# Hybrid decoder block on one core: the room of part 2's small tiles, the MLP's first loads, and where the left operands' combinations are made

## The chip, the core and the metric

The kernel runs on one core of a Trainium2 chip. Its time is the device time of one execution in microseconds (us); a kernel is run several times and the median is given. Five engines work side by side, each on its own queue and in order: TensorE (PE, matmuls into PSUM), VectorE (DVE), ScalarE (ACT), GpSimd (POOL) and SyncE (SP), which here issues all DMAs. They wait for each other through semaphores only.

## The reference

One decoder block on x of 2048 tokens by 1024, float32:

```python
h = _rmsnorm(x, norm_pre_mix)
proj = einsum('bsd,de->bse', h, w_in)          # q, k, v, u, z, two gates
y_attn = _mixer_dilated_attention(q, k, v)     # three dilated windows, softmax-combined
y_gmlp = _mixer_chunked_gmlp(u, z, ...)        # causal mixing in chunks of 128 tokens
merged = gate_a * (y_attn @ w_branch_attn) + gate_b * (y_gmlp @ w_branch_gmlp)
y = merged @ w_out
x = x + _rmsnorm(y, norm_post_mix)
h = _rmsnorm(x, norm_pre_mlp)
a = relu(h @ w_mlp_in)                         # 1024 -> 4096
y = (a * a) @ w_mlp_out                        # 4096 -> 1024
x = x + _rmsnorm(y, norm_post_mlp)
```

## The kernel before

**Numbers.** A float32 operand is split into a high part, rounded to TensorE's `float32r`, and the rest (`split`, lines 66 to 74: ACT, POOL or DVE writes the high part, DVE or POOL subtracts, L75). A product is three matmuls: high by high, high by low, low by high.

**Order.** TensorE's instructions run in the order in which the program writes them (`manual_schedule`). For the other engines and the DMA queue a planner lays out the order with a model of the times; on the chip each queue then runs strictly in that order. A tile that takes the room of older tiles waits for those tiles' last users.

**Part 1** (lines 127 to 715) computes the projections, the attention and the gMLP and leaves them in DRAM: `gate_d`, `ya_d`, `yg_d`. Its last matmuls on TensorE are the z products, which read the second of two `hT` buffers.

**Part 2** (718 to 1037) goes over four chunks of 512 tokens in the order 2, 3, 0, 1. `load_y` loads and splits the chunk's six y tiles. `merge` makes, for each of eight slices dt, two products with `w_branch`, multiplies them by the sigmoid of the gates (`gt`, L753), adds them (POOL, L755) and splits the sum into `mg`. `out_block` multiplies four blocks of 128 tokens by `w_out` (`wo`), adds the residual (`xr`, stored as `x1_d`) after one norm, applies the next norm with the gains `gpost` and `gmlp` (`y1`, L790 to L800), and at its next call (`flush`) transposes the result. Chunks 2 and 0 store the transposes as `h2_d`; chunks 3 and 1 combine them with those of the partner chunk (POOL, L814 to L817) and store five tiles per block, `t_d` (L821, `store`). For chunk 1 these tiles lie in `tail`, which takes the place of the y tiles.

**The MLP** uses Strassen-Winograd's scheme: seven products in place of eight on 2x2 blocks, `TERMS` naming the left and right operand of each. It has two stages.

*First stage* (line 1040 on): for two halves of the tokens and 16 quarters q of `w_mlp_in`, `product` makes seven products of 12 matmuls each. The right operands are `B11`, `B21` (from `h2_d`) and `T1` to `T4`, `B22` (from `t_d`, `load_t`); they stay for a half. The left ones come from pairs of raw tiles `w1r` (`load_a`), combined on POOL and split (`sum_a`: S1 to S4 and A22 into tiles `wl`), or, for the first four and the last three q, as lone halves `ar` (`lone_a`, tag `c`). `places` orders the products: near the ends of a half all products 1 and 2 come ahead, then chains of 6, 7, 5, 4, 3. The results are squared, and at product 3 POOL makes four more combinations (L955 to L961), the left operands of the second stage; seven tiles per (half, q) are stored in `s_d`, laid out as 7 x 128 columns for each block of 128 tokens.

*Second stage* (1101 on): 64 steps n (8 groups g of two q, by 8 blocks), each of seven products of 6 matmuls (`yproduct`). `load_s` loads and splits the two 7 x 128 tiles of a step two steps ahead, in three sets of buffers; `load_w2`, `sum_w2` and `op_w2` make the right operands of the next group in 18 buffers (4 in `r4`, 14 in `bL`). DVE adds each result to the accumulators `acc` (L1204). In the last group `finish` normalizes a chunk's block, adds the residual and stores the output.

**Room.** Pools are stacked. Part 2's pools `yp2`, `gtp`, `mg0`, `wop`, `y1p`, `sm2`, `mg1`, `tp2` all belong to `e2`, which closes after the last block's store (L1045). Only then do the MLP's `bp` (right operands), `wp3` and `cp3` open, over the same room; the second stage's `bL` and `yp3` follow over these.

Of the kernel before, what the change touches and what calls it, by code (L numbers as in the profile page):

```python
# [41 lines left out]
def block_kernel(ctx, tc, a, out):  # L42
# [78 lines left out]
    s_d = dtile([NF // 2, 2, P, 4, 7, P], "sd")  # L121
# [596 lines left out]
    e2 = ExitStack()  # L718
    yp = stack(e2, "yp2", 1)
# [3 lines left out]
    y1p = stack(e2, "y1p", 2)  # L723
    sm = stack(e2, "sm2", 2)
    wo = [wop.tile([P, 2, D], F32R, name=f"wo{k}") for k in range(KT)]

    def load_wo(k):
        raw = y1p.tile([P, D], F32, name=f"woraw{k}", tag="y1")
        split_in(wo[k], a["w_out"][:, k, :], raw, "act")

    def load_y(c, engs=("act", "dve")):
        cs = slice(c * 512, (c + 1) * 512)
        yt = yp.tile([P, 6, 2, 512], F32R, name=f"yt{c}", tag="yt")
        for k in range(6):
            split_in(yt[:, k], ya_d[k, :, cs] if k < 2 else yg_d[k - 2, :, cs], None, *engs)
        return yt

    def merge(c, yt, between, each=None):
        cs = slice(c * 512, (c + 1) * 512)
        mg = []  # L740
        for dt in range(KT):
# [4 lines left out]
            for wch, ks in ((0, range(0, 2)), (1, range(2, 6))):  # L746
# [4 lines left out]
                for k in ks:  # L751
                    mm3(p, wb[k][:, 0, dsl], wb[k][:, 1, dsl], yt[:, k, 0, :], yt[:, k, 1, :], k == ks[0], k == ks[-1])
# [10 lines left out]
    def out_block(c, i, mg):  # L763
# [3 lines left out]
        xt = tp.tile([P, D], F32, name=f"xr_{c}{i}", tag="xr", bufs=1)  # L767
        sp.dma_start(xt, x[t0:t0 + P, :])
        second = c % 2
        if second:  # L770

            tt = tt_tile(c, i)
            for o in range(2):
                sp.dma_start(tt[:, 3 * o], h2_d[:, o * 4:o * 4 + 4, t0 - 512:t0 - 512 + P])
        y1 = y1p.tile([P, D], F32, name=f"y1_{c}{i}", tag="y1")
# [26 lines left out]
        for k in range(0, KT, 4):  # L802
            pt = psum_aux(f"pt_{c}{i}{k}")
            if second:
                ht = tt[:, 4 if k else 2]
# [7 lines left out]
        if second:  # L813
            pool.tensor_sub(tt[:, 0], tt[:, 2], tt[:, 0])  # L814
            pool.tensor_sub(tt[:, 1], tt[:, 4], tt[:, 0])
            pool.tensor_sub(tt[:, 2], tt[:, 4], tt[:, 2])
            pool.tensor_sub(tt[:, 3], tt[:, 3], tt[:, 1])  # L817
        yield
        if second:
            dst = t_d[c // 2].rearrange("p o k t -> p (o k) t")[:, :, i * P:(i + 1) * P]  # L820
            sp.dma_start(dst, tt.rearrange("p o k t -> p (o k) t"))  # L821
# [14 lines left out]
    chunks = (2, 3, 0, 1)  # L836
    e3, er = ExitStack(), ExitStack()
# [11 lines left out]
    b_, a_, araw, bank, xs_, u_, c1_ = {}, {}, {}, {}, {}, {}, {}  # L849
# [40 lines left out]

    def sum_a(half, q):
# [4 lines left out]
        w = {n: wp3.tile([P, 2, 4, P], F32R, name=f"{n}_{half}{q}", tag="wl", bufs=7) for n in names}  # L896
        s1 = wp3.tile([P, 4, P], F32, name=f"s1_{half}{q}", tag="s1", bufs=2)
# [9 lines left out]
    def product(half, q, i):  # L907
# [25 lines left out]
        elif i == 2:  # L933
            c1_[key] = rx.tile([P, 512], F32, name=f"c11_{nm}", tag="c1", bufs=LEAD + 1)
            square(c1_[key], p)
            store_s(0, c1_[key])
        elif i in (6, 7):
            u_[half, q, i] = cp3.tile([P, 512], F32, name=f"u{i}_{nm}", tag=f"u{i}", bufs=3 if i == 6 else 2)
            dve.tensor_add(u_[half, q, i], xs_[key], p)

# [4 lines left out]
        if i in (5, 7) and (half, q, "c") in bank and (half, q, 7) in u_:  # L945
            output(u_[half, q, 7], bank[half, q, "c"])
            store_s(5, u_[half, q, 7])
# [3 lines left out]
        elif i == 3:  # L951
            a11, a12, a21, a22 = c1_[key], xs_[key], u_[half, q, 6], u_[half, q, 7]
            output(a21, p)
            s1, s2, s4 = (cp3.tile([P, 512], F32, name=f"s{n}_{nm}", tag="c", bufs=3) for n in (1, 2, 4))
            pool.tensor_add(s1, a21, a22)  # L955
            store_s(4, s1)
            pool.tensor_sub(s2, s1, a11)
# [34 lines left out]
    def spatial_out(dt):  # L992

        nonlocal tp, gpost, gmlp, ttp
        if dt < 2:
            sz_out(*late.pop(0))
        if dt == 1:
            ez.close()
            mgp.append(stack(e2, "mg1", 1))
            tp = stack(e2, "tp2", 2)  # L1000
            gpost = tp.tile([P, D], F32, name="gpost", bufs=1)
# [294 lines left out]
```

## Time and profile before

| | |
|---|---|
| median of 3 runs | 2868.62 us (2867.49 to 2871.62) |
| the profiled execution | 2863.28 us, span 2861.5 us, mean granted TensorE clock 0.977 |
| busy, share of the span | PE 95%, DVE 55%, ACT 36%, POOL 35% |
| moved by DMA | 475 MB, mean 166 GB/s |

The span goes from the first to the last instruction of one profiled execution. A row of busy time by stretches gives, for each engine, its busy microseconds and its number of instructions in the stretch; then TensorE's granted clock as a share of full speed, the DMA engines' busy share and the GB/s moved. Matmuls overlap in the record, so TensorE's rate is read from the number of matmuls in a stretch rather than from its busy time. A row of the list of waits names the engine and line that waited, what released it, and total, times and longest in us. SPq is SyncE's queue: the row tells when a DMA was issued and how long its issue took, waiting for its turn included.

### The profile page before, as it was taken

What the parts mean: (1) busy time and instruction counts of PE and PEld (TensorE: products, weight loads), DVE (VectorE), ACT (ScalarE), POOL (GpSimd) and SP (SyncE); (2) the same over time, 40 slices, a digit from 0 to 9 for tenths busy, and PEclk for the clock granted to TensorE, in tenths of its full rate; (3) what the DMA queues carried; (4) which work ended last, traced back from release to release, by engine and by line L of the source; (5) the groups of instructions that cost most, each with busy time, mean ns of one, the idle gap of its engine ahead of it and who ended that gap; (6) DMA issues with size and microseconds to landing.
All of it is one profiled execution on the core that took longest, in us unless ns stands there. A gap on an engine that the chain in (4) does not pass through costs nothing. (4 is left out here: it accounts for less than half of the span.)

```text
span 2861.5 us, 36328 instructions
## 1 busy us (share of the span) xinstructions
PE 2729.3 (95%) x13364; PEld 2287.1 (80%) x13364; DVE 1587.3 (55%) x2684; ACT 1039.1 (36%) x2039; POOL 1003.7 (35%) x703
## 2 busy tenths in 40 slices
PE   8999999999999999999996999899997999999996
PEld 8889888988888888787775788677886887888875
DVE  5664462444443353655556544555445676777788
ACT  4213111244443321543444454454444222223332
POOL 0340341200000023213025665546658343344434
PEclk9999999999999999999998999989999999999998
DMA  7544545465666464656467555655556323333345
GB/s 252 176 150 149 173 135 180 142 201 177 203 210 199 163 199 128 204 171 183 143 186 234 155 158 159 191 174 157 157 156 209 117 95 125 126 120 125 127 137 196
DMA packets 348370, 475.38 MB, mean 166 GB/s; under 512 B 19872, under 2 KB 222880, under 8 KB 348192
## 3 DMA queue, kind: packets, MB, share of 16 engines
q1 hardware_dynamic: 348192, 473.06, 52.0%
q8 instruction: 105, 1.72, 0.2%
q14 instruction: 73, 0.60, 0.1%
HBM read 307.11 MB, written 165.87 MB: 165 GB/s over the span
## 5 line engine op out<-in xcount | busy, mean ns | idle before, releaser
L70 ACT ACTIVATE s<-s 128x896 fp32r<-128x896 f32 x128 | 121.9, 953 | 269.8 <-PE ya L1197 137.8
L918 PE MATMUL aa<-B,A 128*128 128x512 f32 x768 | 191.2, 400 | 11.6 <-ACT A L70 9.3
L1204 DVE TENSOR_TENSOR acc<-acc,ya 128x512 f32<-128x512 f32 x224 | 151.4, 683 | 80.2 <-PE ya L1197 79.7
L75 DVE TENSOR_TENSOR s<-s 128x896 fp32r<-128x896 f32 x128 | 169.5, 1326 | 44.6 <-ACT s L70 44.4
L918 PEld LDWEIGHTS aa<-B,A 128*128 128x128 f32 x768 | 146.5, 192 | 47.5 <-ACT A L70 10.5
L72 POOL TENSOR_SCALAR w_g<-w_g_r 128x1024 fp32r<-128x1024 f32 x32 | 34.2, 1068 | 411.2 <-PE g L87 384.8
L85 PE MATMUL x<-hT_a,wq 128*128 128x512 f32 x384 | 149.7, 390 | 0.0
L87 PE MATMUL x<-hT_a,wq 128*128 128x512 f32 x384 | 149.4, 389 | 0.0
L86 PE MATMUL x<-hT_a,wq 128*128 128x512 f32 x384 | 149.4, 389 | 0.0
L603 DVE TENSOR_REDUCE o<-po 128x256 f32<-128x512 f32 x48 | 33.2, 691 | 183.9 <-PE po L602 183.9
L918 PE MATMUL ab<-T_first,S 128*128 128x512 f32 x384 | 96.7, 402 | 24.2 <-ACT T_first L70 15.9
L70 ACT ACTIVATE hl<-r 128x512 fp32r<-128x512 f32 x48 | 30.4, 633 | 231.5 <-POOL r L248 86.7
L1197 PE MATMUL ya<-T2y,s 128*128 128x512 f32 x384 | 100.0, 396 | 13.8 <-ACT s L70 13.8
L75 POOL TENSOR_TENSOR T2y<-w2r,T2y 128x512 fp32r<-128x512 f32 x16 | 20.5, 1306 | 262.4 <-ACT T2y L70 262.4
L1197 PE MATMUL ya<-B11y,s 128*128 128x512 f32 x384 | 103.0, 405 | 9.9 <-DVE acc L1204 9.9
L75 DVE TENSOR_TENSOR A<-w1r,A 128x512 fp32r<-128x512 f32 x68 | 64.8, 953 | 84.5 <-ACT A L70 84.4
L899 POOL TENSOR_TENSOR s<-w1r 128x512 f32<-128x512 f32 x32 | 43.8, 1369 | 191.6 <-DMA w1r<-in_w_mlp_in_dram 183.8
L1197 PE MATMUL yc<-B22y,s 128*128 128x512 f32 x384 | 100.8, 398 | 8.2 <-DVE acc L1204 8.2
L918 PEld LDWEIGHTS ab<-T_first,S 128*128 128x128 f32 x384 | 74.8, 196 | 41.5 <-ACT T_first L70 16.3
L755 POOL TENSOR_TENSOR g<-g,g 128x512 f32<-128x512 f32 x28 | 36.9, 1318 | 195.8 <-DVE v_pm L94 106.5
L85 PE MATMUL g<-hT_b,w_g 128*128 128x512 f32 x256 | 105.6, 412 | 0.0
L75 DVE TENSOR_TENSOR S<-w1r,S 128x512 fp32r<-128x512 f32 x96 | 95.5, 996 | 18.0 <-ACT S L70 17.0
(321 smaller groups left out, 8061.5 us busy)
## 6 DMA issues: line engine op xcount, KB each, us to landing
s<-sd SPq DMA_DIRECT2D x128, 448.0 KB, 3.8
w1r<-in_w_mlp_in_dram SPq DMA_DIRECT2D x64, 512.0 KB, 5.2
qk<-hl SPq DMA_DIRECT2D x24, 1024.0 KB, 5.3
qq<-qk SPq DMA_DIRECT2D x96, 256.0 KB, 4.8
sd<-s SPq DMA_DIRECT2D x96, 256.0 KB, 2.6
w_g_r<-in_w_in_dram SPq DMA_DIRECT2D x32, 512.0 KB, 5.3
gated<-gt SPq DMA_DIRECT2D x64, 256.0 KB, 2.8
g<-gated SPq DMA_DIRECT2D x64, 256.0 KB, 3.8
```

The costliest lines, as they stand in the source:

```text
L70: act.activation(hi, src, AF.Copy)
L72: pool.tensor_scalar(hi, src, 1.0, 1.0, op0=OP.mult, op1=OP.mult)
L75: (pool if lo_eng == "pool" else dve).tensor_sub(lo, src, f32(hi))
L85: pe.matmul(ps, lh, rh, start=start, stop=False)
L86: pe.matmul(ps, lh, rl, start=False, stop=False)
L87: pe.matmul(ps, ll, rh, start=False, stop=stop)
L603: dve.tensor_reduce(ot[:, :, j * 64:(j + 1) * 64], po.rearrange("p (b h e) -> p b e h", b=4, h=2), axis=AX.X, op=OP.add)
L755: (dve if dt == KT - 1 else pool).tensor_add(parts[0], parts[0], parts[1])
L899: pool.tensor_add(s1, a21, a22)
L918: pe.matmul(p, w[:, l, k, :], h[:, r, k, :], start=i in (1, 6, 5) and not k and not n, stop=k == 3 and n == 2, skip_group_check=True)
L1197: pe.matmul(p, s[:, l], w[:, r], start=i in (1, 2, 5) and not m and not o, stop=m == 1 and o == 2, skip_group_check=True)
L1204: dve.tensor_add(an, an, p)
```

## The change

Five things change. No matmul is added or left out.

1. **Room in part 2.** A pool `bot`, opened first and closed only in the MLP's second stage, holds the small tiles: `gpost`, `gmlp`, two `y1`, six separate y tiles `yt0` to `yt5`, and `xr`. `gtp`, `mg0`, `wop` and `mg1` lie above it in `e2`, which now closes before the MLP's first product. For chunk 1 the five tiles of a block lie in three `yt` tiles each and are stored by three DMAs instead of one. The first lone halves are loaded into gate tiles.
2. **The MLP's tiles in that room.** The first stage's `wl` tiles go to `yt0` to `yt5` and `gmlp` in turn, `s1` to `gpost` (one buffer, before two), and `u6` with `u7` to `y1` and `xr`. `ar` has two buffers of its own; `c1` has 2 in place of 5.
3. **The MLP's start.** T2, the raw pair of q 0, T3, T1 and the pair of q 1 are loaded before the first product in the program's order; (2,1) joins the four products ahead of the last block's transposes; T4 and B22 follow its store.
4. **The left operands' combinations** leave the first stage: `s_d` holds four tiles per (half, q) instead of seven. In the second stage `load_s` loads raw tiles three steps ahead, and `sum_s`, two steps ahead, splits three of them, makes the four combinations on POOL for both q at once, and splits these in two pieces.
5. **The second stage's room and end.** `acc` lies at the bottom, the first tiles of `bL` are given places by hand, and `finish` handles both chunks of a block together, when all seven of its products are added.

```diff
+    e2b, e2 = ExitStack(), ExitStack()
+    bot = stack(e2b, "bot", 1)
+    sm = stack(e2b, "sm2", 2)
+    gpost = bot.tile([P, D], F32, name="gpost")
+    gmlp = bot.tile([P, D], F32, name="gmlp")
...
-        yt = yp.tile([P, 6, 2, 512], F32R, name=f"yt{c}", tag="yt")
+        yt = [bot.tile([P, 2, 512], F32R, name=f"yt{c}{k}", tag=f"yt{k}") for k in range(6)]
...
-            raw = cp3.tile([P, 512], F32, name=f"ar{n}_{half}{q}", tag="c", bufs=3)
-            raw = raw.rearrange("p (k c) -> p k c", k=4)
+            raw = wp3.tile([P, 4, P], F32, name=f"ar{n}_{half}{q}", tag="ar", bufs=2)
...
+    WL, n_wl = ("yt0", "yt1", "yt2", "yt3", "yt4", "yt5", "gmlp"), [0]
...
         elif i == 3:
-            a11, a12, a21, a22 = c1_[key], xs_[key], u_[half, q, 6], u_[half, q, 7]
+            a21 = u_[half, q, 6]
             output(a21, p)
-            s1, s2, s4 = (cp3.tile([P, 512], F32, name=f"s{n}_{nm}", tag="c", bufs=3) for n in (1, 2, 4))
-            pool.tensor_add(s1, a21, a22)
-            store_s(4, s1)
-            pool.tensor_sub(s2, s1, a11)
-            store_s(2, s2)
-            pool.tensor_sub(a21, a11, a21)
             store_s(3, a21)
-            pool.tensor_sub(s4, a12, s2)
-            store_s(6, s4)
...
-    for q, i in ((0, 1), (1, 1), (0, 2), (1, 2)):
-        product(first_half, q, i)
-    flush()
-    store()
     e2.close()
     ea = ExitStack()
     bp = stack(ea, "bp", 1)
     wp3 = stack(ea, "wp3", 1)
-    cp3 = stack(ea, "cp3", 1)
+
+    tt_ = {n: bp.tile([P, 2, 4, 512], F32R, name=f"{n}_first", tag=n, bufs=1) for n in ("B22", "T4", "T1", "T3", "T2")}
+    load_t(first_half, "T2", tt_["T2"])
+    load_a(first_half, 0)
+    load_t(first_half, "T3", tt_["T3"])
+    load_t(first_half, "T1", tt_["T1"])
+    load_a(first_half, 1)
+    for q, i in ((0, 1), (1, 1), (0, 2), (1, 2), (2, 1)):
+        product(first_half, q, i)
+    flush()
+    store()
+    for name in ("T4", "B22"):
+        load_t(first_half, name, tt_[name])
...
     def load_s(n):
...
+        sraw_[n] = r4.tile([P, 2, 4, P], F32, name=f"sraw_{n}", tag="sraw", bufs=2)
+        for m in range(2):
+            sp.dma_start(sraw_[n][:, m], s_d[2 * g + m, half][:, i])
+
+    def sum_s(n):
...
+        raw = sraw_.pop(n)
+        split(w[:, 0, :, :3], w[:, 1, :, :3], raw[:, :, :3], "act", "dve")
+        a11, a12, a22, a21 = (raw[:, :, k] for k in range(4))
+        pool.tensor_add(a22, a21, a22)
+        pool.tensor_sub(a21, a11, a21)
+        pool.tensor_sub(a11, a22, a11)
+        pool.tensor_sub(a12, a12, a11)
+
+        for to, k in (((3, 7, 3), (0, 2, 1)), ((4, 6, 1), (2, 4, 1))):
+            to, k = slice(*to), slice(*k)
+            split(w[:, 0, :, to], w[:, 1, :, to], raw[:, :, k], "act", "dve")
...
     ea.close()
-    bL = stack(e3, "bL", 1)
+    e2b.close()
     yp = stack(e3, "yp3", 1)
     sm = stack(e3, "sm3", 2)
-    for j in range(2, 7):
+    bL = stack(e3, "bL", 1)
...
+    for tag, sh in [("wl10", 0), ("wl11", 0), ("wl12", 0), ("wl13", 0), ("s2", 1), ("wl6", 0), ("wl7", 0), ("wl8", 0),
+                    ("wl9", 0), ("wl2", 0), ("wl3", 0), ("wl4", 0), ("wl5", 0), ("wl0", 0), ("wl1", 0), ("s1", 1)]:
+        place[tag] = bL.tile([P, 2, 2, 7, P] if sh else [P, 2, 512], F32R, name=f"{tag}_first", tag=tag)
...
-            left[n, ci] = left.get((n, ci), 4 if not ci else 3) - 1
-            if not left[n, ci]:
-                finish(half, b, ci)
+            left[n] = left.get(n, 7) - 1
+            if not left[n]:
+                finish(n)
...
         if i == 1:
-            if n + 2 < len(ysteps):
-                load_s(n + 2)
+            sum_s(n + 2)
+            load_s(n + 3)
```

More of the change, by code (lines that the diff above doesn't have):

```diff
@@ L943, in output @@
             square(t, t)
[L945 removed]
+        if i in (5, 7) and (half, q, "c") in bank and (half, q, "7") in u_:
             output(u_[half, q, 7], bank[half, q, "c"])
[L947 removed]
+            store_s(2, u_[half, q, 7])
         elif i == 4:
@@ L1023, in block_kernel @@
             store()
-            if n == 3 and i == 0:
-                tail = yp.tile([P, 48, P], F32, name="tail", tag="yt")
             b = out_block(c, i, mg)
@@ L1199, in yproduct @@
         ci, nh = {1: (0, 0), 2: (0, 0), 6: (0, 1), 3: (0, 1), 4: (1, 0), 7: (1, 1), 5: (1, 1)}[i]
-        if not g and (half, b, ci) not in acc:
-            acc[half, b, ci] = yp.tile([P, D], F32, name=f"acc{half}{b}{ci}", tag=f"acc{half}{b}{ci}")
         an = acc[half, b, ci][:, nh * 512:(nh + 1) * 512]
```

165 lines of the change are left out of this document (93 added, 72 removed).

## The prediction

> **What bounds the kernel now.** I read the page's first line, then TensorE's list of waits, then busy time by stretches, and only then the timeline of single stretches.
>
> ```profile
> span 2861.5 us, 36328 instructions
> ```
>
> All terms below are made against this profiled execution: span 2861.5 us, its own time 2863.28 us. The median of the three runs shown is 2868.62, 5.3 us more; I add that at the end.
>
> ```profile
> PE ab L918 <- DVE u L939: 16.3, 5, 4.4
> PE ab L918 <- ACT T_first L70: 15.9, 1, 15.9
> PE ya L1197 <- ACT s L70: 13.8, 1, 13.8
> PE ya L1197 <- DVE acc L1204: 12.6, 7, 2.7
> PE b L85 <- DVE g L753: 10.4, 5, 4.4
> PE aa L918 <- ACT A L70: 9.3, 2, 5.5
> ```
>
> These are TensorE's waits over the whole run (total, times, longest, in us). They sit at changes of stage, not in the steady parts: one where the MLP begins (`T_first`), one where its second stage begins (`s`), some inside the first stage (`u`, `A`), and the rest near the end (`acc`). The next view is busy time by stretches; behind PE stands the number of matmuls, behind POOL's the granted clock, the DMA share and GB/s.
>
> ```profile
> 1500.00:1550.00 50.00, 27.19 (x114) 20.84 (x113) 27.01 (x31) 17.91 (x32) 27.35 (x20) 0.80 0.77 259
> 1510.00:1520.00 10.00, 9.22 (x43) 7.01 (x42) 3.25 (x7) 5.22 (x12) 4.67 (x4) 1.00 1.02 310
> 1600.00:1650.00 50.00, 46.36 (x192) 37.62 (x191) 29.43 (x34) 26.57 (x46) 33.44 (x23) 0.93 0.50 146
> 1650.00:1700.00 50.00, 50.00 (x221) 41.19 (x220) 25.01 (x33) 26.07 (x43) 31.08 (x22) 1.00 0.50 149
> 1800.00:1850.00 50.00, 43.49 (x184) 34.97 (x182) 28.04 (x30) 25.98 (x40) 27.40 (x18) 0.97 0.59 190
> 1850.00:1900.00 50.00, 38.05 (x133) 29.65 (x134) 27.29 (x27) 22.59 (x35) 18.74 (x11) 0.80 0.63 201
> 1900.00:1950.00 50.00, 45.87 (x198) 37.55 (x198) 30.65 (x37) 22.99 (x40) 31.83 (x22) 0.96 0.46 137
> 2150.00:2200.00 50.00, 35.87 (x157) 29.02 (x155) 26.39 (x25) 26.66 (x44) 44.74 (x31) 0.92 0.67 215
> 2444.00:2463.00 19.00, 18.70 (x83) 15.03 (x82) 15.40 (x18) 6.11 (x9) 18.48 (x12) 1.00 0.48 175
> ```
>
> A full stretch of 50 us holds 221 matmuls (the row at 1650), so one costs 0.226 us, a first-stage product (12) 2.7 us and a second-stage step (42) 9.5 us. What a stretch lacks is lost, its slow clock included. At 1500 it lacks 107: 24 us. At 1600, 1800, 1850 and 1900 it lacks 29 + 37 + 88 + 23 = 177: 40 us. At 2150 it lacks 64: 14.5 us. These 78 us are what the change can win.
>
> The granted clock is 0.80 in the two worst stretches and 1.00 in the full ones. The Trainium skill ("TensorE: Matmul & The Clock Gate", "What's actually happening") says that a gate halves TensorE's clock after an idle window of about 3.4 us; the two rows agree.
>
> **Part by part. The first loads of the MLP (a).**
>
> ```profile
> 1499.98 0.40 PE L87 MATMUL o<-wo,mg 128*128 128x512 f32 x1
> ```
> ```profile
> 1520.91 0.52 SPq L821 DMA_DIRECT2D td<-tail  x1
> 1521.47 4.01 SPq L888 DMA_DIRECT2D w1r<-in_w_mlp_in_dram  x2
> 1525.53 1.14 SPq L81 DMA_DIRECT2D T_first<-td  x2
> ```
>
> The first row is TensorE's last product with `w_out`; the others are SyncE's queue. T2 is asked for at 1525.5, behind the last block's store, though TensorE was done with `w_out` at 1500.4. In the changed program everything that the last norm still uses (`y1`, `xr`, `tt`, the two gains) lies in `bot`, and T2, T3, T1 and two pairs of `w_mlp_in` take the room of `gt`, `mg` and `wo` alone. So they may be issued some 20 us earlier, and a fifth product, (2,1), moves ahead of the last transposes as cover.
>
> If T2, the first pair and the three lone halves that follow (1 + 1 + 0.75 MiB) go first, they take 2.9 MB / 310 GB/s = 9 us from about 1502. TensorE is covered to 1502 + 5 x 2.7 + 1 (transposes) = 1517: nothing is left of the stall. If SyncE issues all that comes earlier in the program (T2, T3, T1, T4, B22: 5 MiB; two pairs: 2; the last blocks' stores and loads: about 2) ahead of product (3,1)'s lone half, that is 9.7 MB or 31 us, plus some 3 us for a split: ready near 1536, and 19 of the 24 us stay. Neither order is shown; I take the middle, **-13** (bounds -24 and -5).
>
> **Inside the first stage (b).** Four POOL operations and three stores per (half, q) go.
>
> ```profile
> L957 POOL TENSOR_TENSOR s<-s,c 128x512 f32<-128x512 f32 x32 | 53.8, 1683 | 2.4
> ...
> L955 POOL TENSOR_TENSOR s<-u,u 128x512 f32<-128x512 f32 x32 | 43.1, 1345 | 58.3 <-ACT u L928 50.4 <-DVE B L75 7.9
> ...
> L634 POOL TENSOR_TENSOR A<-A 128x1024 f32<-128x1024 f32 x3 | 7.2, 2384 | 0.2
> ```
> ```profile
> SPq L924 <- POOL s L955: 11.5, 3, 5.8
> ```
> ```profile
> 1880.54 0.40 SPq L81 DMA_DIRECT2D ar<-in_w_mlp_in_dram  x1
> ```
> ```profile
> 1886.55 0.80 PE L918 MATMUL aa<-B,A 128*128 128x512 f32 x1 [5.46 <-ACT A L70]
> ```
>
> The four lines (the dearest and the cheapest stand above) took 32 x 4 x 1.35 to 1.68 = 172 to 215 us of POOL. More important is what stood behind them. SyncE issues in order; between 1820 and 1900 its `sd` stores waited 11.5 us for L955, with `ar` loads behind them; one issued at 1880.5 reached TensorE as a wait of 5.5 us. Also `ar` shared three `c` tiles with these sums and now has two of its own; DVE's splits lose a competitor on POOL. Against it: other waits here are in-order queues held by a load (B's, A's) that no POOL sum delays, and `c1` shrinks from 5 buffers to 2. Its store follows at once, so I cost that at nothing; without that cover a product waits for one store. Bounds -40 and -5; I take 5/8 of the loss, **-25**.
>
> **Between the stages (c).** Before, the first operands of `w_mlp_out` in `bL` (T2y, T3y) and `s` get the room of B22 and of tiles beside it, and B22 is read by the very last product of the first stage; hence the 13.8 us on `s`. The list with `place` gives them the room of `w1r`, T2, T3 and T1, whose last products come earlier in the last chain, and `s` 0 and its sums need only `r4`. POOL's 31 operations in the row at 2150 lose the combinations; 4 sums per step come instead. I take **-13** of 14.5 (bounds -14.5 and -6).
>
> **Second stage, steady (d).** DMAs shrink from 448 to 256 KB and are issued one step earlier; on POOL, 64 x 4 operations of 128x256 are added. From 2384 ns at 1024 elements and 1345 at 512, an estimate for 256 is 0.83 us: 3.3 us per step of 9.5. DVE and ACT split the same elements in three pieces instead of two.
>
> ```profile
> L75 DVE TENSOR_TENSOR s<-s 128x896 fp32r<-128x896 f32 x110 | 143.4, 1304 | 34.7 <-ACT s L70 34.5
> L1204 DVE TENSOR_TENSOR acc<-acc,ya 128x512 f32<-128x512 f32 x192 | 130.0, 684 | 75.5 <-PE ya L1197 74.9
> ```
> ```profile
> 1538.99 1.75 DVE L75 TENSOR_TENSOR A<-w1r,A 128x512 fp32r<-128x512 f32 x1
> 1540.66 2.28 DVE L75 TENSOR_TENSOR T_first<-T_first 128x1024 fp32r<-128x1024 f32 x1
> 1542.87 0.68 DVE L75 TENSOR_TENSOR S<-w1r,S 128x512 fp32r<-128x512 f32 x1
> 1543.47 1.21 DVE L75 TENSOR_TENSOR T_first<-T_first 128x1024 fp32r<-128x1024 f32 x1
> ```
> ```profile
> 1540.27 1.59 POOL L902 TENSOR_TENSOR w1r<-w1r 128x512 f32<-128x512 f32 x1
> ```
>
> DVE per step now: 7 x 0.684 + 2 x 1.304 = 7.4 us. Until 1541.9, with POOL at work, a 512 subtraction took 1.75 us and a 1024 one 2.28; right after, 0.68 and 1.21. So one piece costs 0.68 to 1.75 (512) and, on the same line, 0.95 to 2.0 (768). New sum per step: 4.8 + 2.3 = 7.1 alone, 4.8 + 5.5 = 10.3 with POOL always in the way; with the share of today's waits about 7.8, under 9.5. So hidden, except at the seven changes of group, where POOL is full (18.48 of 19 us in the row at 2444, 12 operations) and a new chain DVE, POOL, ACT, DVE must pass through it. I take 0.9 us at each: **+6** (bounds -4, since shorter pieces can free a bank sooner (`acc`), and +31, rival three).
>
> The Trainium skill ("SBUF — State Buffer", "Who interferes with whom") says that a DVE operation with two SBUF inputs and a POOL operation exclude each other for the whole instruction. The rows agree: both lengths lose the same 1.07 us, a wait that fits into one POOL operation (1.59 us), not a share of their length. By that rule three pieces pay three waits where two paid two, which speaks against this change; it is rival three.
>
> **The tail (e).** `finish` handles both chunks of a block at once.
>
> ```profile
> L103 DVE TENSOR_TENSOR r_fin<-r_fin,t_fin 128x1 f32<-128x1 f32 x16 | 7.9, 496 | 0.1
> L98 DVE SCALAR_TENSOR_TENSOR t_fin<-r_fin,v_fin 128x1 f32<-128x1 f32 x16 | 6.5, 410 | 0.2
> L1178 DVE TENSOR_TENSOR fs<-fs 128x1 f32<-128x1 f32 x14 | 5.7, 408 | 0.8 <-ACT jk L1176 0.8
> ```
>
> DVE bounds the last eight steps (the `acc` waits). Per step twelve tiny operations become seven: two such as above (0.44) go and three with one input, which I put at a third of that: 1.3 us, 10.6 in all. Added: one more split piece and POOL's 3.3 us per step beside its multiplies, so more waits in all two-input operations; I put that at 12. **+2** (bounds -8, +12).
>
> **Start of part 2 (f).**
>
> ```profile
> 1126.90 0.91 SPq L748 DMA_DIRECT2D g<-gated  x2
> ```
> ```profile
> 1146.11 0.40 PE L85 MATMUL b<-yt,wb 128*128 128x512 f32 x1
> ```
>
> By the order of the pools, `gt` and `y1` move from room that was free by 1126.9 to that of the second `hT` buffer, which the z products read until part 2's first product at 1146.1. So 1 MiB of gates and 1 MiB of `w_out`, issued from 1126.9, come 19 us later, into a merge that already waits for `g`. Two MiB at 310 GB/s are 7 us, partly in time when SyncE idles: **+3** (bounds -1, +8).
>
> Sum: -13 - 25 - 13 + 6 + 2 + 3 = -40. 2863.3 - 40 = 2823.3; plus 5.3: **2829 us**.
>
> **Rivals.** One: the loads only move the wait. DMA volume, not the last norm, sets when the MLP starts, and b's waits are loads in order; then a gives 3, b 5, c 13, costs 11: -10, 2859. For it: 310 GB/s at a DMA share of 1.02 before T2 was even asked for. Against: SyncE stood still with that work unissued.
>
> Two, slower: the new chain at the group changes. `sum_s` for the next step needs its S2 within 12 products of 1.36 us (16.3 us) after its tile falls free; if POOL's 12 queued operations (18.5 us) go first, then 4 x 0.83 and two splits (2.6), it is 8 us late, in-order DVE stands with it, and TensorE restarts at a low clock (2 more). Seven times 10 is 70: -51 + 5 + 70 = +24, 2893. It decides from 46 / 7 = 6.6 us per change on. Against it: between those changes POOL has room, and today `u`'s sums passed through a POOL 60% busy (31.08 of 50 at 1650) without a lost matmul.
>
> Three: DVE becomes the bound of the second stage, 10.3 a step. Today a step takes about 540/55 = 9.8 (the group rows above are of 2210 to 2750, with 110 pieces, two a step), so 56 x 0.55 = 31, and 10 more in the tail: -51 + 3 + 31 + 12 = -5, 2864. Against: it needs POOL busy always, and 4.3 + 3.3 of 9.5 is 80%.
>
> Four, it doesn't do what it says: as one, with c lost too; I count it within one.
>
> **How the numbers follow.** Forecast 0.60, own range 2800 to 2858 (all bounds added up would give 2777 to 2904; ends rarely meet). Rival one 0.15, two 0.15, three 0.10. The range 2800 to 2868 leaves out two and a little at both ends. A measurement tells about 0.2% (5.7 us) from no change. Faster: nearly all of the forecast, 0.11 of one, 0.04 of three: 0.74. Same: 0.03 of one, 0.05 of three, 0.01: 0.09. Slower: 0.17.
>
> **What would show it.** a: T2 issued before 1510, over 190 matmuls from 1500 to 1550 (counted from the same last `wo` product). b: `sd` stores waiting for no POOL line; over 205 matmuls in each of the four stretches. c: no wait on `s` above 2 us. d: DVE's two-input pieces under 1.2 us on average and no TensorE wait on `s` at group changes; POOL's sums near 0.83 us. f: the first merge within 5 us of now. The forecast is wrong if (3,1) or (0,6) waits over 15 us, or if TensorE lacks over 3 us per group in the second stage.

## The result, and the profile after

The changed kernel takes 2974.5 us (median of 4 runs, 2972.4 to 2977.7) against 2870.1 for the kernel before (4 runs): a ratio of 1.037, 95% interval 1.035 to 1.038. It is 104 us slower; the forecast was 2829, the range 2800 to 2868. The profiled execution took 2977.66 us, 114 more than that of before. Each experiment below was measured together with the kernel before, whose median differs a little from set to set (2861.3 to 2865.3); ratios are to that median, and kernels of different sets are compared by how far they lie from it.

First the page's first line, then TensorE's list of waits, whole run (total, times, longest in us):

```profile
span 2975.6 us, 36211 instructions
```
```profile
PE yc L1247 <- DVE acc L1252: 98.5, 23, 9.3
PE aa L928 <- ACT A L70: 22.7, 1, 22.7
PE b L85 <- DVE g L755: 11.4, 6, 4.4
PE ya L1247 <- DVE acc L1252: 9.7, 5, 3.6
PE ya L1247 <- DVE acc L1255: 7.9, 2, 5.7
PE ab L928 <- DVE u L953: 5.6, 1, 5.6
```

The waits on `s` and on `T_first` are gone, as the change meant. In their place stand 98.5 us on `acc` (12.6 before, the largest row on `acc`) and 22.7 us on a lone half. Busy time by stretches shows where (behind PE the number of matmuls):

```profile
1500.00:1550.00 50.00, 25.77 (x108) 20.72 (x106) 33.47 (x40) 24.33 (x39) 24.45 (x18) 0.77 0.89 296
1600.00:1650.00 50.00, 50.00 (x217) 40.62 (x216) 25.48 (x35) 25.93 (x44) 16.52 (x12) 1.00 0.41 121
...
1850.00:1900.00 50.00, 50.00 (x218) 40.78 (x218) 27.70 (x34) 29.94 (x48) 10.99 (x8) 1.00 0.58 185
...
2150.00:2200.00 50.00, 39.37 (x139) 30.66 (x140) 21.18 (x30) 21.91 (x37) 25.84 (x23) 0.83 0.39 122
```
```profile
2480.00:2500.00 20.00, 12.35 (x42) 9.72 (x42) 7.58 (x11) 3.67 (x6) 19.69 (x18) 0.83 0.12 38
2500.00:2520.00 20.00, 17.05 (x66) 13.74 (x67) 13.22 (x20) 3.91 (x6) 5.97 (x8) 0.83 0.18 52
2520.00:2540.00 20.00, 20.00 (x89) 16.37 (x88) 13.75 (x21) 4.54 (x7) 7.24 (x10) 1.00 0.18 53
```

Three things are to be seen. Inside the first stage no stretch lacks much any more (184, 133 and 198 matmuls in three of them before), but a full stretch now holds 217 or 218 matmuls, not 221. In the second stage a full stretch of 20 us holds 89, the one at 2480 only 42, with POOL busy 19.69 of 20 us, DVE 7.58, and the granted clock at 0.83 there: the head of a group, where the next group's operands are begun. And the start at 1500 is no better than before (114); counted over 50 us from each kernel's last product with `w_out`, it holds 88 matmuls against 114.

From the starts of all matmuls in each trace one can take the time of a part, less 0.2267 us for each matmul in it. What is left is TensorE's loss (us). The parts are the first 144 matmuls of the MLP's first stage (counted from the last product with `w_out`, so the last transposes are in it), the next 2256, the last 288, the second stage's groups, and what follows the last matmul:

| kernel | part 2 ends at | start | inside first stage | its last 288 | group 1 | groups 2 to 7 | group 8 | behind |
|---|---|---|---|---|---|---|---|---|
| before | 1500.0 | 28.2 | 44.7 | 1.7 | 17.7 | 13.3 | 25.8 | 11.9 |
| after | 1506.8 | 35.0 | 11.1 | 10.2 | 26.6 | 116.4 | 35.3 | 16.0 |
| e1, sums on DVE | 1505.2 | 34.8 | 11.1 | 3.9 | 13.4 | 37.8 | 30.0 | 14.5 |
| e2, order of w_mlp_out's work | 1503.0 | 34.8 | 11.1 | 10.2 | 15.8 | 29.5 | 33.8 | 16.0 |
| e3, right operands moved | 1501.7 | 34.2 | 2.3 | 9.1 | 26.5 | 116.3 | 36.5 | 15.0 |
| e4, combinations in the first stage | 1506.4 | 32.3 | 38.0 | 1.6 | 21.0 | 16.8 | 29.5 | 16.0 |
| e5, e2 and early lone halves | 1500.2 | 31.6 | 11.1 | 9.6 | 15.8 | 27.9 | 36.5 | 14.9 |
| e8, e5 and all operands moved | 1506.1 | 29.2 | 0.0 | 9.0 | 16.8 | 24.9 | 33.9 | 16.0 |
| e10, e8 with the old end | 1499.5 | 30.3 | 0.0 | 8.9 | 16.8 | 23.5 | 42.5 | 11.8 |
| e11, e10 and order at the start of the second stage | 1498.4 | 31.6 | 0.0 | 0.2 | 16.7 | 23.5 | 42.5 | 11.8 |
| e13, e8 and that order | 1502.5 | 29.3 | 0.0 | 0.2 | 16.3 | 26.3 | 35.5 | 14.9 |

Of the 114 us, groups 2 to 7 make 103: 17.2 us more in each of the six. The inside of the first stage gives 34 back. Group 8, in which nothing is prepared for a next group, loses 9.5 more.

**What stands at the head of a group.** The next four fences are the timeline of POOL, ACT, DVE and PE in the changed kernel; in brackets the idle time before a row and what ended it.

```profile
2478.02 1.30 POOL L75 TENSOR_TENSOR B11y<-w2r,B11y 128x512 fp32r<-128x512 f32 x1 [4.66 <-PE ya L1247]
2479.27 0.72 POOL L1168 TENSOR_TENSOR sraw<-sraw 128x256 f32<-128x256 f32 x1
...
2490.30 2.07 POOL L75 TENSOR_TENSOR B21y<-w2r,B21y 128x512 fp32r<-128x512 f32 x1
2492.33 1.28 POOL L1139 TENSOR_TENSOR w2r<-w2r 128x512 f32<-128x512 f32 x1
...
2496.19 1.27 POOL L1142 TENSOR_TENSOR w2r<-w2r 128x512 f32<-128x512 f32 x1
2497.42 0.72 POOL L1168 TENSOR_TENSOR sraw<-sraw 128x256 f32<-128x256 f32 x1
```
```profile
2477.31 0.63 ACT L70 ACTIVATE B11y<-w2r 128x512 fp32r<-128x512 f32 x1 [5.61 <-DMA w2r<-in_w_mlp_out_dram]
2477.84 0.61 ACT L70 ACTIVATE B21y<-w2r 128x512 fp32r<-128x512 f32 x1
2481.93 0.63 ACT L70 ACTIVATE s<-sraw 128x512 fp32r<-128x512 f32 x1 [3.47 <-POOL sraw L1169]
```
```profile
2474.14 1.27 DVE L1252 TENSOR_TENSOR acc<-acc,ya 128x512 f32<-128x512 f32 x2
2482.59 1.07 DVE L75 TENSOR_TENSOR s<-sraw,s 128x512 fp32r<-128x512 f32 x1 [7.18 <-ACT s L70]
2483.59 0.67 DVE L1252 TENSOR_TENSOR acc<-acc,yc 128x512 f32<-128x512 f32 x1
...
2499.64 0.69 DVE L75 TENSOR_TENSOR s<-sraw,s 128x512 fp32r<-128x512 f32 x1 [7.24 <-ACT s L70]
```
```profile
2477.85 1.56 PE L1247 MATMUL ya<-T4y,s 128*128 128x512 f32 x6
2484.41 2.90 PE L1247 MATMUL yc<-B22y,s 128*128 128x512 f32 x6 [5.00 <-DVE acc L1252]
...
2502.95 2.93 PE L1247 MATMUL yc<-B22y,s 128*128 128x512 f32 x6 [6.19 <-DVE acc L1252]
```

Read upwards: PE waits for a bank that an addition to `acc` has to empty; the addition stands in DVE's queue behind a split of `s`; the split waits for its high part on ACT, that for the sums on POOL, and these stand behind POOL's part of B11, which has no data yet: its raw tile came late (ACT's 5.61 us). POOL's row names PE as what ended its wait, but its input was written by ACT at 2477.94. Some 15 us later it happens again: POOL works through the operands and sums of `w_mlp_out` first, the next sums begin at 2497.4, and PE waits 6.19 us. So each group pays twice.

The first links of this were to be seen in the trace of before, in the timeline of POOL and of ACT:

```profile
2444.23 1.29 POOL L75 TENSOR_TENSOR B11y<-w2r,B11y 128x512 fp32r<-128x512 f32 x1 [4.48 <-ACT B11y L70]
```
```profile
2443.52 0.63 ACT L70 ACTIVATE B11y<-w2r 128x512 fp32r<-128x512 f32 x1 [7.25 <-DMA w2r<-in_w_mlp_out_dram]
```

POOL stood 4.5 us there as well; nothing that TensorE needed soon was queued behind it.

The granted clock is 0.83 in the two stretches that hold the waits and 1.00 in the next. By the Trainium skill ("TensorE: Matmul & The Clock Gate", "What's actually happening") an idle window of some 3.4 us halves the clock; the waits of 5.00 and 6.19 us and the rows at 2480 and 2500 agree.

### The profile page after: what moved, and what is told of

Its sections match the earlier page's. It is cut to its first block, busy times and chain, and to the rows that moved or that the text cites. A ratio compares the mean times of both kernels' runs of the same rounds, so it can differ in the third digit from the quotient of the medians.

```text
span 2975.6 us, 36211 instructions
## 1 busy us (share of the span) xinstructions
PE 2767.9 (93%) x13364; PEld 2308.9 (78%) x13364; DVE 1546.9 (52%) x2708; ACT 1047.9 (35%) x2095; POOL 984.8 (33%) x831
## 4 chain that ended last, share of the span: by engine, by line
PE 69%; POOL 12%; DMA 7%; issue 4%; DVE 4%; ACT 2%; SPq 0%; DVEq 0%; POOLq 0%; ACTq 0%
PE ab L928 9%; PE aa L928 6%; PE ac L928 6%; PE ya L1247 5%; PE g L87 4%; PE g L85 4%; PE g L86 4%; PE yc L1247 3%; PE x L85 3%; PE x L87 3%; PE x L86 3%; PE pv L596 2%; DMA g<-gated 1%; PE o L87 1%; PE o L85 1%
## 5 line engine op out<-in xcount | busy, mean ns | idle before, releaser
L70 ACT ACTIVATE s<-sraw 128x768 fp32r<-128x768 f32 x186 | 130.7, 703 | 496.9 <-POOL sraw L1169 234.2
L75 DVE TENSOR_TENSOR s<-sraw,s 128x768 fp32r<-128x768 f32 x186 | 159.0, 855 | 265.5 <-ACT s L70 265.2
L928 PE MATMUL aa<-B,A 128*128 128x512 f32 x768 | 190.5, 401 | 26.9 <-ACT A L70 22.7
L1247 PE MATMUL yc<-B22y,s 128*128 128x512 f32 x336 | 107.9, 465 | 87.8 <-DVE acc L1252 87.8
L72 POOL TENSOR_SCALAR w_g<-w_g_r 128x1024 fp32r<-128x1024 f32 x32 | 33.6, 1050 | 410.4 <-PE g L87 328.8
L1247 PEld LDWEIGHTS yc<-B22y,s 128*128 128x128 f32 x336 | 73.4, 225 | 113.2 <-DVE acc L1252 64.9
L85 PE MATMUL o<-wo,mg 128*128 128x512 f32 x256 | 102.6, 401 | 5.6 <-ACT mg L70 4.8
L1168 POOL TENSOR_TENSOR sraw<-sraw 128x256 f32<-128x256 f32 x64 | 47.0, 734 | 183.3 <-DVE s L75 182.4
L70 ACT ACTIVATE S<-w1r 128x512 fp32r<-128x512 f32 x96 | 60.3, 629 | 131.8 <-PE ac L928 79.8
L85 PE MATMUL g<-hT_a,w_g 128*128 128x512 f32 x256 | 104.4, 408 | 0.0
L757 POOL TENSOR_TENSOR g<-g,g 128x512 f32<-128x512 f32 x28 | 36.5, 1305 | 200.7 <-DVE v_pm L94 105.9
L87 PE MATMUL o<-wo,mg 128*128 128x512 f32 x256 | 101.8, 398 | 0.4 <-DVE mg L75 0.4
```

The costliest lines, as they stand in the source:

```text
L70: act.activation(hi, src, AF.Copy)
L75: (pool if lo_eng == "pool" else dve).tensor_sub(lo, src, f32(hi))
L85: pe.matmul(ps, lh, rh, start=start, stop=False)
L87: pe.matmul(ps, ll, rh, start=False, stop=stop)
L757: (dve if dt == KT - 1 else pool).tensor_add(parts[0], parts[0], parts[1])
L928: pe.matmul(p, w[:, l, k, :], h[:, r, k, :], start=i in (1, 6, 5) and not k and not n, stop=k == 3 and n == 2, skip_group_check=True)
```

## The experiments

Two theories stood at first. **Q** (queues): the loss comes from what stands ahead of what in the in-order queues of POOL, ACT and DVE. **D** (load): DVE is the bound of the second stage, by more pieces and by POOL in its way. `tc.issue_after(x)` puts what follows behind x in the queue of x's engine and adds no wait.

### e1: the sums on DVE

```diff
-        pool.tensor_add(a22, a21, a22)
+        dve.tensor_add(a22, a21, a22)
...
```

> The changed kernel, with the four sums per step of the second stage on DVE instead of POOL; nothing else moves. Theory Q (queues): at a change of group the sums stand in POOL's queue behind the operands of w_mlp_out, ACT's and DVE's splits stand behind the sums, the additions to acc behind the splits. Then the cause goes with the POOL sums: 2880 to 2925 us, TensorE's waits on acc under 40 us in all (98.5 now on yc alone). Theory D (DVE is the bound of the second stage, three pieces and POOL's lock): DVE gets 4 x 0.4 = 1.6 us per step more to do: 2975 to 3010 us, the waits on acc as now or longer.

2867.9 us, ratio 1.0011 (1.0001 to 1.0020). Better than either had it: DVE takes on the four sums, and the kernel lies 2.6 us above the one before of its set, where the changed one lay 104 above. D falls. TensorE's waits on the additions in e1:

```profile
PE ya L1247 <- DVE acc L1252: 24.5, 20, 2.6
```
```profile
PE yc L1247 <- DVE acc L1252: 13.2, 8, 2.8
```

No single one is above 2.8 us. A third row on `acc`, the first copies into it (L1255), is 8.9 us here and 7.9 in the changed kernel.

### e2 and e12: the same work in another order

```diff
...
-            if more and at == 2:
-                for j in range(2):
-                    ops_of(g + 1, j)
-            if more and at == 3:
-                for q in (2 * g + 2, 2 * g + 3):
-                    sum_w2(q)
+            if more and at in (2, 3):
+                with tc.issue_after(last_sum[0]), tc.issue_after(last_act[0]):
+                    for j in range(2):
+                        op_w2(2 * g + at, OPS[j])
+            if more and at in (4, 5):
+                with tc.issue_after(last_sum[0]):
+                    sum_w2(2 * g + at - 2)
```

`last_sum` and `last_act` are the step's last sum on POOL and last high part on ACT. In the changed kernel the planner had laid all of this work close together near the head of the group: it runs from 11.5 to 31 us behind the group's first matmul, in e2 from 30 to 65 us, with the sums of later steps in between.

> The changed kernel, with one thing other: on POOL and ACT the low and high parts of B11 and B21 and the sums of w_mlp_out for the next group are queued behind the sums and splits of s of the steps 2 to 5 of a group, a few per step, in place of all together at the head of the group. No work is added or taken away. Theory Q: the two waits of 4.9 and 6.2 us per group near 2480 and 2495 go, 7 x 9 to 13 us: 2885 to 2925 us. Theory D: the same load on DVE and POOL, only elsewhere: 2965 to 2985 us.

2872.8 us, 1.0027 (1.0017 to 1.0036), better than Q's range. Not one instruction is added or gone, and the kernel lies 7.4 us above the one before, not 104: 97 us go by order alone. The same stretches by busy time in e2:

```profile
2480.00:2500.00 20.00, 18.32 (x79) 14.33 (x78) 13.49 (x19) 7.62 (x13) 18.31 (x16) 1.00 0.18 52
2500.00:2520.00 20.00, 19.30 (x83) 15.14 (x82) 13.31 (x21) 5.80 (x10) 12.98 (x14) 1.00 0.43 159
```

POOL is nearly as full (18.31 us against 19.69), TensorE has 79 matmuls in place of 42, the clock stays at 1.00. A group takes 80.9 us (median of groups 2 to 7; 95.6 in the changed kernel, 78.2 before).

e12 leaves out `tc.issue_after(last_act[0])`, so that only POOL's order differs.

> The kernel of e2 with POOL's order alone changed; ACT takes the high parts of B11 and B21 where it took them in the changed kernel, ahead of the splits of the sums. If POOL's queue alone made the loss: as e2, 2868 to 2878 us. If ACT's queue, which stood 5.6 us for the raw w_mlp_out ahead of those splits, makes part of it, 3 to 6 us come back at each of seven changes of group: 2890 to 2915 us.

2879.0 us, 1.0062 (1.0045 to 1.0079). Between the two branches. One row of e12's waits, 2250 to 2750:

```profile
ACT B11y L72 <- DMA w2r<-in_w_mlp_out_dram: 47.2, 12, 5.7
```

ACT still stands for the raw tile ahead of the splits, and by the starts of TensorE's matmuls that costs 6.6 us more than in e2 in groups 2 to 7, about one per group, less than the second branch had it: POOL's queue is the cause, ACT's a small part.

### e6: DVE's order alone

```diff
...
+        if i == 3:
+            with tc.issue_after(last_add[0]):
+                split_sums(n + 2)
```

`split_sums` is the second half of `sum_s`, the two splits of the sums; `last_add` is the step's last addition to `acc`.

> The changed kernel, with one thing other: on DVE (and nowhere else) the two splits of the sums are queued behind the step's last addition to acc, so that in-order DVE no longer stands before a POOL sum while additions are ready behind it. POOL's and DVE's work is the same. Theory Q: the chain gets some 3 to 4 us more before it holds an addition; of 14 us per group about 8 go: 2900 to 2935 us, DVE's idle time on ACT's s under 150 us between 2250 and 2850 (211 now). Theory D: 2965 to 2985 us.

2932.6 us, 1.0237 (1.0219 to 1.0254). In range, near its end. DVE's waits from 2250 to 2850, in the changed kernel and in e6:

```profile
DVE s L75 <- ACT s L70: 218.8, 135, 7.3
```
```profile
DVE s L75 <- ACT s L70: 54.2, 23, 6.5
```

DVE's standing for ACT falls from 219 to 54 us, yet the kernel still lies 67 us above the one before: 37 of the 104 us are all that go; the sums are as late as they were at the head of a group, and a wait of 6.5 us still holds what follows the split. DVE's place in the queue passes the delay on; it doesn't make it.

### e4: the combinations in the first stage again

```diff
...
-            a21 = u_[half, q, 6]
+            a11, a12, a21, a22 = c1_[key], xs_[key], u_[half, q, 6], u_[half, q, 7]
             output(a21, p)
+            pool.tensor_add(a22, a21, a22)
+            store_s(4, a22)
+            pool.tensor_sub(a21, a11, a21)
             store_s(3, a21)
+            pool.tensor_sub(a11, a22, a11)
+            store_s(2, a11)
+            pool.tensor_sub(a12, a12, a11)
+            store_s(6, a12)
...
```

> The changed kernel with part 4 undone: the combinations are made in the first stage again, in place (no tiles c), seven tiles per (half, q) go through DRAM, the second stage loads and splits them as before; room, first loads and end as in the change. Both theories: the second stage takes 666 us again in place of 785, so 2855 to 2885 us. Inside that, if the inner stalls of the first stage came from the sums and their stores, they are back (40 us in the first stage, TensorE lacks over 100 matmuls between 1600 and 2000): 2880 to 2895; if from the lone halves' shared tiles, they stay away: 2850 to 2865.

2880.8 us, 1.0059 (1.0038 to 1.0081): the branch in which the stalls come from the sums and their stores. Stretches of e4, and one row of its SyncE waits between 1800 and 1900:

```profile
1600.00:1650.00 50.00, 45.38 (x187) 36.47 (x186) 28.34 (x32) 23.11 (x40) 31.42 (x23) 0.93 0.56 163
...
1850.00:1900.00 50.00, 43.73 (x172) 34.54 (x171) 28.63 (x26) 26.49 (x40) 24.05 (x16) 0.90 0.73 241
```
```profile
SPq L934 <- POOL u L969: 23.7, 4, 8.2
```

Most of the stalls of before are back, with the lone halves' own buffers kept, and SyncE's stores stand for POOL again. So part 4 does win in the first stage what it was meant to: 38.0 against 11.1 us of loss.

### e11: the start of the second stage

```diff
-    for j in range(2):
-        ops_of(0, j)
-    for q in range(2):
-        sum_w2(q)
     sum_s(0)
+    with tc.issue_after(last_sum[0]):
+        for j in range(2):
+            ops_of(0, j)
+        for q in range(2):
+            sum_w2(q)
```

> The kernel of e10, and at the start of the second stage the sums of the first step stand ahead of B11, B21 and the sums of w_mlp_out in POOL's queue, in place of behind them. Theory Q for the change of stage: DVE's wait of 8.4 us on the first sums goes, and with it TensorE's wait of 6.1 us on u at the end of the first stage: 4 to 7 us less than e10. If the first operands of w_mlp_out are then late instead: no gain, and a wait on them at the first product of the second stage.

2847.7 us, 0.9954 (0.9939 to 0.9969), against 2855.6 for e10 on the same chip: 7.9 less. One row of DVE's waits from 2095 to 2185, in e10 and then in e11:

```profile
DVE s L77 <- ACT s L72: 12.9, 7, 8.4
```
```profile
DVE s L77 <- ACT s L72: 7.4, 9, 1.3
```

The 8.4 us are gone, and the loss in the first stage's last 288 matmuls falls from 8.9 to 0.2. It was the same queue: the first sums stood behind twelve operations on `w_mlp_out`, DVE behind them, and the additions to `u` behind DVE.

### e5: the start of the MLP

```diff
...
     for q, i in ((0, 1), (1, 1), (0, 2), (1, 2), (2, 1)):
         product(first_half, q, i)
+        if i == 1 and q < 2:
+            lone_a(first_half, 3 - q, q)
...
```

T3, T1 and the second raw pair are loaded behind this loop.

> The kernel of the run e2 (w_mlp_out's work spread over the steps), and the lone halves of (3,1) and (2,2) asked for right after T2 and the first raw pair, ahead of T3, T1, the second pair, T4 and B22. If SyncE's order ahead of the half of (3,1) makes the 22.7 us wait at the MLP's start, as rival one's mechanism in the prediction's part a had it, the wait falls to 5 to 10 us (the next is S2 of q 0, whose tile is freed by the last blocks' stores): 2857 to 2864 us against 2873. If the splits on ACT and DVE bound the start, the wait stays over 18 us: 2869 to 2875.

2867.2 us, 1.0014 (1.0002 to 1.0026), above the 2857 to 2864 expected: it lies 2.9 us above the kernel before of its set, e2 7.4. TensorE's timeline in e5:

```profile
1523.10 2.98 PE L930 MATMUL aa<-B,A 128*128 128x512 f32 x12
1533.05 4.68 PE L930 MATMUL ab<-T_first,S 128*128 128x512 f32 x12 [6.97 <-ACT S L72]
1537.57 2.91 PE L930 MATMUL aa<-B,A 128*128 128x512 f32 x12
1547.93 1.22 PE L930 MATMUL aa<-B,A 128*128 128x512 f32 x2 [7.46 <-ACT A L72]
```

(3,1) runs right behind the transposes, so SyncE's order made the wait of 22.7 us. But two waits of 7 us follow, on S2 of q 0 and on the third lone half, and the start's loss falls only from 34.8 to 31.6: the 22.7 us are mostly moved, not won. In the changed kernel ACT's splits into S wait for the stores of the last blocks, whose room those tiles share (ACT's timeline):

```profile
1533.07 0.63 ACT L70 ACTIVATE S<-w1r 128x512 fp32r<-128x512 f32 x1 [1.29 <-DMA td<-tt]
```

That this shared room bounds the start wasn't tried by itself.

### e3 and e9: where the operands lie

TensorE's slower rate inside the first stage had no wait behind it. Timeline of the changed kernel, steady part:

```profile
2005.32 2.94 PE L928 MATMUL ab<-T,S 128*128 128x512 f32 x12
2008.10 2.96 PE L928 MATMUL ab<-T,A 128*128 128x512 f32 x12
```

A product starts 2.78 us after the one ahead, 2.72 before the change. By the programs' layout, the right operands T1 to T4 and B22 began at 128 modulo 512 bytes of a partition before, and so did their left ones; in the changed kernel the right ones begin at 0. **Theory A** says that this sets the rate.

```diff
+    bp.tile([P, 32], F32, name="pad")
     wp3 = stack(ea, "wp3", 1)
```

> The changed kernel with 128 unused bytes per partition ahead of the MLP's right operands, so that T1 to T4 and B22 begin, like their left operands, at 128 modulo 512 bytes of a partition (0 against 128 in the change); no instruction differs. Theory A (addresses): TensorE's interval in those products goes from 232 back to 227 ns, as before the change; 1920 of them take 9 us less, a steady 50 us of the first stage holds 220 or 221 matmuls instead of 217: 2961 to 2969 us. Theory L (load: the lower rate comes from what the other engines do, or from the chip): 217 stays, 2970 to 2979 us.

2961.1 us, 1.0339 (1.0317 to 1.0361): 96.8 us above the kernel before of its set, 7.6 less than the changed kernel's 104.4. The same part of the timeline, and a stretch, in e3:

```profile
2003.11 2.88 PE L928 MATMUL ab<-T,S 128*128 128x512 f32 x12
2005.83 2.88 PE L928 MATMUL ac<-T,S 128*128 128x512 f32 x12
```
```profile
1650.00:1700.00 50.00, 50.00 (x221) 41.19 (x220) 24.42 (x31) 25.48 (x42) 16.52 (x12) 1.00 0.32 97
```

2.72 us and 221 again, and the inside of the first stage loses 2.3 us in place of 11.1. The other way round, in the kernel before, with 384 unused bytes ahead of the left operands:

```diff
     wp3 = stack(ea, "wp3", 1)
+    wp3.tile([P, 96], F32, name="pad")
```

> The kernel before with 384 unused bytes per partition ahead of the left operands' pool, so that the left operands of those five products begin at 0 and the right ones at 128 modulo 512; no instruction differs. Theory A: 227 becomes 232 ns in 1920 matmuls, 9 us more than before the change (ratio 1.003). Theory L: the same as before, within 3 us.

The time hardly moves: 2866.8 us, 1.0009 (0.9998 to 1.0020), but the rate does. A full stretch of e9:

```profile
1650.00:1700.00 50.00, 50.00 (x217) 40.66 (x217) 25.24 (x30) 24.83 (x41) 32.10 (x23) 1.00 0.57 167
```

The mean interval in the five products is 232 ns, as expected, while the inside of the first stage loses 46.4 us, only 1.7 more than in the profile of before. The waits on `u` are 11.3 us in all against 16.3; so the slower matmuls seem to have filled stalls that come from the queues. That reading is argued, not shown.

### e8, e10 and e13: what can be kept

e8 is e5 with the pad of e3 and 64 unused bytes at the top of the other side of the room, so that left and right operands of all the MLP's products are at equal places modulo 512, and these are multiples of 128.

> The kernel of e5 with every left and right operand of the MLP at equal places modulo 512 bytes (128 bytes ahead of the right operands as in e3, 64 at the top of the other side of the room). Theory A: 9 us less in the first stage's five products, some 2 in the other two, some 4 in the second stage (233, 232 and 231 ns become 229 and less in 1100 of 2688 matmuls): 2842 to 2852 us, a ratio to the kernel before of 0.992 to 0.995. Theory L: as e5.

2851.4 us, 0.9961 (0.9947 to 0.9975): in the range by its time, just above it by its ratio. The mean interval is 226.7 ns in all products of the first stage (226.8 in B11 and B21, 229 to 230 before) and 226.7 to 228.7 in the second; the first stage's inside loses nothing.

e10 takes e8 and puts the end of before back (`finish` for each chunk).

> The kernel of e8 with the end as before the change: a chunk's block is normalized and stored as soon as its own products are added (four and three of seven), in place of both together. Theory E (the joint end packs four POOL multiplications and four DVE operations per step into the chain of the sums): the last group loses 26 us in place of 34, as before the change, and the piece behind the last matmul 12 in place of 16: 2838 to 2845 us. Theory S (the sums alone crowd the last group, whatever the end): 2849 to 2855.

A miss: 2855.6 us, 0.9985 (0.9973 to 0.9996), slower than e8. The last group loses 42.5 us with it, against 33.9, and the piece behind the last matmul 11.8 against 16.0. So with the sums in the second stage the joint end is worth some 4 us. Without them it isn't: e4 has the joint end and no sums, and loses 29.5 and 16.0 us there, 7.8 more than the kernel before.

e13 is e8 with the order of e11.

> The kernel of e8 (joint end kept) with the order at the start of the second stage of e11. The two are in different stages, so their gains should add up: e8's 2851.4 less the 7.9 us that e11 won on e10: 2841 to 2846 us, a ratio to the kernel before of 0.992 to 0.995. If the gain at the start is taken back by the fuller last group (34 us lost there against 42 with the end by chunk), 2847 to 2851.

2845.2 us, 0.9929 (0.9916 to 0.9943). It beats both kernels: 20 us below the one before, where the changed one lay 104 above.

## Why the prediction was wrong, by its own steps

**d, the step that failed.** "Hidden, except at the seven changes of group ... I take 0.9 us at each." It is 17.2 us in each of groups 2 to 7, 103 of the profile's 114 us, and e2, by order alone, takes 87 of them away. The mechanism was written down as rival two, with a chance of 0.15 and 10 us per change, and its condition (over 6.6 us) holds. Two arguments put it too low. That POOL has room between the changes is true and of no use: the planner put the work close together near the head of the group, and the queue runs in that order. That `u`'s sums passed through a POOL 60% busy was no evidence: what stood behind those were stores, here additions stand behind DVE. And its price counted one delay; there are two, the first from a wait for a raw tile that the trace of before showed.

Rival three is out. The two shapes of DVE's splits in the changed kernel, 2250 to 2750:

```profile
L75 DVE TENSOR_TENSOR s<-sraw,s 128x512 fp32r<-128x512 f32 x84 | 64.2, 764 | 175.9 <-ACT s L70 175.5
L75 DVE TENSOR_TENSOR s<-sraw,s 128x768 fp32r<-128x768 f32 x43 | 42.9, 998 | 6.3 <-ACT s L70 6.3
```

A step has 2 x 0.764 + 0.998 = 2.53 us of them, against 2 x 1.304 = 2.61 before, far from the 5.5 of that rival. (Its price has a slip too: from 9.8 to 10.3 us are 0.5 per step, not 0.55.) The test "under 1.2 us on average" held. POOL's four sums took 0.73, 0.74, 0.79 and 1.00 us on average in the same stretch, 0.82 over all, against the estimate of 0.83: the durations were right, and the order was what counted.

**b was right, and larger.** -25 forecast; the stalls inside the first stage went altogether, and no store of `sd` waits for POOL any more. The loss fell by 33.6 us, and 8.8 of what is left is the rate (e3), so the stalls were worth some 42. How much of that the sums and their stores made can be read from three kernels at the same slower rate: 46.4 us of loss in e9 (nothing changed but the rate), 38.0 in e4, 11.1 in the changed kernel. So part 4 makes 27 of these 35 us; the other 8 come from the rest of the change, and e4 has no wait left of the kind `A` from ACT that cost 9.3 us inside the stage before.

**a was wrong.** -13 forecast, +7 measured. T2 was asked for at 1508.5, as the test wanted, but 88 matmuls ran in the 50 us in place of over 190; the half of (3,1) came behind the last block's stores, T4 and B22, and 22.7 us were waited: the case in which 19 us stay ("ahead of product (3,1)'s lone half"), and over the 15 us named as a sign of being wrong. SyncE's queue in the changed kernel:

```profile
1508.50 0.93 SPq L81 DMA_DIRECT2D T_first<-td  x2
```
```profile
1543.21 0.99 SPq L81 DMA_DIRECT2D ar<-in_w_mlp_in_dram  x2
```

e5 shows this order to be one cause; with it mended, the next operands are late, as rival one had it. A wait of 4.2 us for ACT to empty a bank, ahead of the third product (0.4 us in the kernel before), was not foreseen either; its cause stays open.

**c was wrong.** -13 forecast. No wait on `s` above 2 us was left, as the test wanted, but the first stage's end and group 1 together lose 17.4 us more. e11 shows 8.7 of it to be the sums' place in POOL's queue (without sums on POOL, in e1 and e4, the end loses 3.9 and 1.6 us). Group 1 holds a change of group too: e2's order takes 10.8 off it. That is d's mechanism again. What then stays, 15.8 us in group 1, is hardly less than the 17.7 of before: the wait on `s` gave way to others, 7.9 us of them on the first copies into `acc`, and why those are late was not tried.

**e** was set at +2 (bounds -8 and +12) and is 9.5 in the last group and 4.1 behind it, 13.6. Its two halves don't add up as they were set. With the old end the sums cost 16.6 us (e10 against before, pads and order included), with the joint end 5.8 (the changed kernel against e4); the joint end saves 4.4 beside the sums (e10 against e8) and costs 7.8 without them (e4 against before). So the sums' share, set at 12, is of the right sign, and the joint end's saving holds only beside them.

**f** can't be told from nothing. The first merge begins at 1143.0 us, 3.1 earlier, as its test allowed; part 2 ends between 1498.4 and 1506.8 us in twelve profiles with the changed part 2, and at 1500.0 and 1505.3 in two with the old one. From its first product to its last, part 2 takes 357.1 to 363.8 us in the twelve (363.8 in the changed kernel's own) and 353.9 and 358.4 in the two: the +3 is neither shown nor excluded.

## What to carry to other kernels

An engine's busy share says whether work fits, its queue says when it runs: before moving work that TensorE waits for soon onto an engine, list what stands ahead of it there, and count that engine's waits, the harmless ones too, since they become the new work's waits. Where a planner lays out the order, the step at which the program names a piece of work may not be where it lands; look at the built order, and pin it where it matters. Order alone was worth 97 us here, more than anything that the change won.

## What the runs showed of the hardware that was not expected

TensorE's rate depends on where its two operands lie. For 128x512 matmuls of `float32r`, mean interval (gaps above 250 ns left out) by the start of the right and the left operand modulo 512 bytes of a partition:

| right, left | interval, ns | runs |
|---|---|---|
| 128, 128 | 226.6 to 227.4 | before, e3, e8 (first stage) |
| 384, 384 | 226.8 | e8 (B11, B21) |
| 448, 448 | 228.4 to 230.1 | before, after, e3, e9 (B11, B21) |
| 0, 128 | 232.0 to 232.5 | after |
| 128, 0 | 231.9 to 232.6 | e9 |
| 448, 128 or 384 | 231.2 to 231.3 | before, after, e3, e9 (second stage) |
| 128 or 384, 448 | 233.1 | before, after, e3, e9 (second stage) |

Of the pairs measured, equal places at 128 or 384 are the fastest, 0 with 128 costs 2.4%. In the second stage, where waits are mixed in, equal places at 128 or 384 come to 227.2 (e8) to 229.0. In the first stage it is the rate of stretches without a single wait, at a granted clock of 1.00; e3 and e9, which differ from their kernels by the unused bytes alone, show the address to be the cause. The Trainium skill ("SBUF — State Buffer", "Who interferes with whom") gives TensorE two independent read ports, one for the moving operand and one for the weight load, and says that it never waits on anyone; these runs differ from what one would conclude from that, and the measurement decides. What in the memory makes it was not tried.
